# Loading x two batches at a time in a batched matmul: 32 KB per partition in one transfer, and transposes that serve both batches

## The chip, the cores and the metric

The kernel runs on one core of a Trainium2 chip. The metric is device time in microseconds (us) of one execution. The kernel before falls on two levels, 516.4 and 517.5 us, so differences under 1 us between two medians say little. The profile is one execution with the hardware profiler on; its span is 1.5 to 2 us shorter than the timed run.

Names used below: TensorE does matmuls and transposes, VectorE (DVE in the profile) and ScalarE (ACT) copy out of PSUM (the on-chip memory that TensorE writes to; the tiles of x, weights and outputs lie in another, SBUF), and GpSimd (POOL) issues most transfers. They run on sixteen DMA engines. SyncE (SP) has a second queue to the same engines. A *packet record* is one row of the trace's list of packets: start, duration, bytes written, queue. On the GpSimd queue one record is one partition's contiguous piece of a transfer.

## The reference

```python
batch, m, k, n = 32, 512, 1024, 768
x = np.random.randn(batch, m, k).astype(np.float32)
weight = np.random.randn(batch, k, n).astype(np.float32)
out = np.matmul(x, weight).astype(np.float32)
```

Per batch that is 2.10 MB of x, 3.15 MB of weight and 1.57 MB of output. Over 32 batches 218.1 MB go over HBM, the memory that holds x, weight and output.

## The kernel before

Each batch's x and weight come in one transfer each on the GpSimd queue, which casts them to bf16. TensorE transposes x in pairs of bf16 (viewed as fp32), VectorE copies the result out of PSUM, and the matmuls follow. Weights have four buffers, x has five, outputs seven. The parts that matter here, with cuts marked:

```python
w_pool = ctx.enter_context(tc.tile_pool(name="w", bufs=4))
x_pool = ctx.enter_context(tc.tile_pool(name="x", bufs=5))
...
out_pool = ctx.enter_context(tc.tile_pool(name="out", bufs=7))
tpsum = ctx.enter_context(tc.tile_pool(name="tpsum", bufs=2, space=bass.MemoryType.PSUM))
...
def load_x(b):
    xs[b] = x_pool.tile([P, MT, K], BF16, name="x_sb")
    nc.gpsimd.dma_start(out=xs[b], in_=x_view[b])
...
def transpose(b, mt):
    pt = tpsum.tile([P, JT, P], F32, name="pt")
    pairs = xs[b].bitcast(F32)
    for j in range(JT):
        nc.tensor.transpose(pt[:, j, :], pairs[:, mt, j::JT], ident)
    xT = xT_pool.tile([P, JT, P, 2], BF16, name="xT")
    nc.vector.tensor_copy(xT..., pt.bitcast(BF16)...)      # both flat: 1024 bf16
    return xT
...
# the first x, in fp32, on the SyncE queue; its last quarter in 16 pieces of 6 rows
# and one of 32
nc.sync.dma_start(x_first[:, :MT - 1], x_view[0, :, :MT - 1])
for block in range(0, 96, 24):
    for at in range(block, block + 4):
        few = slice(at, block + 24, 4)
        nc.sync.dma_start(x_first[few, MT - 1], x_view[0, few, MT - 1])
nc.sync.dma_start(x_first[96:, MT - 1], x_view[0, 96:, MT - 1])
load_w(0)
...
for b in range(1, AHEAD):          # AHEAD = 3
    load_x(b)
    load_w(b)
load_x(AHEAD)
for b in range(B):
    if b + AHEAD + 1 < B:
        load_x(b + AHEAD + 1)
    if b + AHEAD < B:
        load_w(b + AHEAD)          # from b = 1 on it waits until batch b - 1 is done
    ...                            # output of batch b - 1, on the GpSimd queue
    # transposes of tiles 0 and 1, then matmuls with those of tiles 2 and 3 between them
```

So before batch 0 is done the queue holds w0 to w3 and x1 to x5. Nothing else can be issued until the matmuls of batch 0 free the first weight buffer.

## Time and profile before

| | before |
|---|---|
| time, median | 517.36 us (516.3 to 517.5, 6 runs) |
| span of the profiled run | 515.7 us |
| HBM traffic over the span | 218.1 MB, 423 GB/s |
| TensorE busy | 417.8 us, 81% |

The list of waits of the kernel before (who waited for whom: us in total, times, longest):

```profile
POOL w_sb L62 <- PE pm L101: 66.2, 8, 35.2
...
PE pm L101 <- DMA w_sb<-in_weight_dram: 43.9, 17, 4.4
```

TensorE waits for weights.

The windows view of the kernel before, at the start and for the long middle. The columns are the window and its length, busy time (instructions) of PE, weight loads, DVE, ACT and POOL, the granted clock, the mean share of the DMA engines and GB/s. Packets of one engine overlap a little in the records, so a full engine reads 1.02.

```profile
40.00:54.00 14.00, 13.59 (x90) 9.41 (x91) 5.23 (x8) 2.34 (x4) 1.06 (x2) 1.00 1.04 219
54.00:61.00 7.00, 6.95 (x47) 4.75 (x46) 1.98 (x3) 1.28 (x3) 0.54 (x1) 1.00 1.02 214
61.00:70.00 9.00, 8.64 (x57) 5.76 (x57) 2.67 (x4) 1.65 (x3) 1.06 (x2) 1.00 1.01 249
70.00:470.00 400.00, 350.35 (x2119) 231.06 (x2157) 107.57 (x163) 62.63 (x107) 42.76 (x81) 0.95 1.02 264
```

The timeline of the kernel before (start us, duration us, what, and in brackets the idle time and what ended it): the first transposes on TensorE, and the moment at which w4 can be issued.

```profile
33.57 3.89 PE L83 MATMUL pt<-ident,x_first 128*128 128x128 f32 x16 [33.57 <-DMA x_first<-in_x_dram]
...
51.08 0.53 POOL L62 DMA_DIRECT2D w_sb<-in_weight_dram  x1 [35.18 <-PE pm L101]
```

The transfer queued last before w4 (x5) lands between 60.6 and 64.5 us, depending on the engine, so w4, issued at 51.1, comes 9 us before the first engine needs it.

### The profile page before, as it was taken

The numbers are of one execution on the slowest core, as the hardware profiler recorded it, in microseconds if no ns is written. First come the engines' busy times: TensorE is split into PE (matmuls) and PEld (weight loads), VectorE is DVE, ScalarE is ACT, GpSimd is POOL, SyncE is SP. The second block draws the span as 40 slices with busy tenths as digits, with TensorE's granted clock in tenths as the row PEclk, the third lists the DMA queues.
The fourth block names the chain that finished last, engine by engine and source line by source line (L and its number), as shares of the span: only waits on it lengthen the run. The fifth ranks groups of instructions, "written<-read, shape, count | busy, mean of one in ns | idle before, by whom it ended". The sixth has DMA issues, their size and how long they took to land.

```text
span 515.7 us, 5952 instructions
## 1 busy us (share of the span) xinstructions
PE 417.8 (81%) x2528; PEld 276.1 (54%) x2576; DVE 129.9 (25%) x196; ACT 76.2 (15%) x129; POOL 51.7 (10%) x102
## 2 busy tenths in 40 slices
PE   0039999999999988779879779887898976999990
PEld 0036666666666655446546455554564644566660
DVE  0023333333333313122223231322331322133330
ACT  0001111111111111111101111110110111111110
POOL 3000111111001010100101001100111010111000
PEclk9999999999999989899979998898997998899996
DMA  8999999999999999999999999999999999999996
GB/s 234 223 225 216 218 272 275 260 243 270 277 274 268 243 261 278 275 273 248 250 275 276 275 259 244 271 274 276 272 240 260 277 275 272 250 244 214 300 426 257
DMA packets 15097, 135.64 MB, mean 263 GB/s; under 512 B 1760, under 2 KB 1760, under 8 KB 3552
## 3 DMA queue, kind: packets, MB, share of 16 engines
q0 software_dynamic: 13824, 126.88, 96.7%
q1 hardware_dynamic: 1248, 8.39, 4.1%
q8 instruction: 20, 0.33, 0.2%
q14 instruction: 5, 0.04, 0.0%
HBM read 167.77 MB, written 50.33 MB: 423 GB/s over the span
## 4 chain that ended last, share of the span: by engine, by line
DMA 63%; PE 30%; DVE 3%; issue 1%; ACT 0%; POOLq 0%
PE pm L101 27%; DMA w_sb<-in_weight_dram 25%; DMA out_dram<-out_sb 16%; DMA x_sb<-in_x_dram 16%; DMA x_first<-in_x_dram 6%; PE pt L70 2%; DVE out_sb L113 1%; DVE xT L72 1%; PE pt L83 1%; ACT out_sb L114 0%; POOLq L144 0%; POOLq L62 0%; POOLq L56 0%
## 5 line engine op out<-in xcount | busy, mean ns | idle before, releaser
L101 PE MATMUL pm<-w_sb,xT 128*128 128x256 bf16 (+1 forms) x2000 | 363.4, 336 | 51.3 <-DMA w_sb<-in_weight_dram 43.9
L101 PEld LDWEIGHTS <-xT 128*128 128x128 bf16 x2048 | 204.5, 101 | 185.8 <-issue 52.9
L72 DVE COPY xT<-pt 128x1024 bf16<-128x1024 bf16 x124 | 82.9, 689 | 204.3 <-PE pt L70 204.3
L112 ACT COPY out_sb<-pm 128x512 f32<-128x512 f32 x64 | 37.5, 585 | 289.0 <-PE pm L101 289.0
L113 DVE COPY out_sb<-pm 128x512 f32<-128x512 f32 x64 | 44.0, 687 | 128.1 <-PE pm L101 128.1
L70 PEld LDWEIGHTS pt<-ident,x_sb 128*128 128x128 f32 x496 | 72.3, 206 | 6.0 <-issue 0.8
L70 PE MATMUL pt<-ident,x_sb 128*128 128x128 f32 x496 | 74.6, 284 | 0.0
L114 ACT COPY out_sb<-pm 128x512 f32<-128x512 f32 x64 | 37.5, 586 | 137.3 <-PE pm L101 137.2
L62 POOL DMA_DIRECT2D w_sb<-in_weight_dram x37 | 19.8, 534 | 155.7 <-PE pm L101 66.2
L56 POOL DMA_DIRECT2D x_sb<-in_x_dram x31 | 16.5, 532 | 172.9 <-DMA w_sb<-in_weight_dram 115.8
L83 PE MATMUL pt<-ident,x_first 128*128 128x128 f32 x32 | 6.0, 349 | 33.6 <-DMA x_first<-in_x_dram 33.6
L144 POOL DMA_DIRECT2D out_dram<-out_sb x28 | 15.0, 536 | 94.4 <-DMA x_sb<-in_x_dram 57.0
L83 PEld LDWEIGHTS pt<-ident,x_first 128*128 128x128 f32 x32 | 5.0, 202 | 34.2 <-issue 33.5
L84 DVE CAST xT<-pt 128x512 bf16<-128x512 f32 x8 | 5.6, 727 | 40.9 <-PE pt L83 40.7
L112 ACT ACT_TABLE_LOAD x1 | 1.3, 1283 | 0.7 <-PEq L195 0.7
masks.py:199 POOL TENSOR_SCALAR_AFFINE_SELECT ident<-ident 128x128 f32<-128x128 f32 x1 | 0.3, 287 | 0.1
masks.py:197 POOL MEMSET ident<- 128x128 f32 x1 | 0.2, 223 | 0.0
L195 POOL MEMSET const-float32-0.0<- 128x1 f32 x1 | 0.1, 98 | 0.2 <-issue 0.2
L195 POOL MEMSET const-bfloat16-1.0<- 128x1 bf16 x1 | 0.1, 101 | 0.0
L195 POOL MEMSET const-uint8-127<- 128x1 uint8 x1 | 0.1, 101 | 0.0
L195 POOL MEMSET const-float32-1.0<- 128x1 f32 x1 | 0.1, 98 | 0.0
## 6 DMA issues: line engine op xcount, KB each, us to landing
w_sb<-in_weight_dram POOLq DMA_DIRECT2D x28, 1536.0 KB, 43.2
out_dram<-out_sb POOLq DMA_DIRECT2D x28, 1536.0 KB, 41.9
x_sb<-in_x_dram POOLq DMA_DIRECT2D x31, 1024.0 KB, 39.6
w_sb<-in_weight_dram POOLq DMA_DIRECT2D x7, 768.0 KB, 31.4
out_dram<-out_sb SPq DMA_DIRECT2D x4, 768.0 KB
out_dram<-out_sb SPq DMA_DIRECT2D x2, 1536.0 KB
x_first<-in_x_dram SPq DMA_DIRECT2D x1, 1536.0 KB
w_sb<-in_weight_dram POOLq DMA_DIRECT2D x2, 384.0 KB, 28.1
```

Source lines behind the costliest of these rows:

```text
L56: nc.gpsimd.dma_start(out=xs[b], in_=x_view[b])
L62: nc.gpsimd.dma_start(out=ws[b][:, at:at + n, :], in_=w_view[b, :, at:at + n, :])
L70: nc.tensor.transpose(pt[:, j, :], pairs[:, mt, j::JT], ident)
L72: nc.vector.tensor_copy(xT.rearrange("p j m r -> p (j m r)"), pt.bitcast(BF16).rearrange("p j m -> p (j m)"))
L83: nc.tensor.transpose(pt[:, i, :], x_first[:, mt, JT * h + i::KT], ident)
L84: nc.vector.tensor_copy(xT[:, 2 * h:2 * h + 2].rearrange("p j m r -> p j r m"), pt.rearrange("p (j r) m -> p j r m", r=2),)
L101: nc.tensor.matmul(pm[bank][:, at:at + size], xT[:, ko // 2, :, ko % 2], ws[b][:, ko, off:off + size], start=(ko == 0 and not (together an ...
L112: nc.scalar.copy(o[:, 0:512], pm[0])
L113: nc.vector.tensor_copy(o[:, 512:1024], pm[1])
L114: nc.scalar.copy(o[:, 1024:N2], pm[2])
L144: nc.gpsimd.dma_start(out=out_view[at], in_=outs[at])
L195: nc = _bacc.Bacc("TRN2", target_bir_lowering=False, num_devices=1)
```

## The change

The intent: fewer and larger pieces for x. Batches 1 to 30 are loaded two at a time. Partition q then holds eight contiguous rows of one of the two batches (32 KB of fp32 in HBM), so 64 partitions belong to each batch. One transpose of a tile serves both batches, and the copy out of PSUM interleaves two tiles, so that the matmuls see the layout as before. The x pool shrinks from five single buffers to two double ones, and all transposes of a pair now stand ahead of its matmuls. The core of the diff, with cuts:

```diff
-    x_pool = ctx.enter_context(tc.tile_pool(name="x", bufs=5))
-    xT_pool = ctx.enter_context(tc.tile_pool(name="xT", bufs=8))
+    x_pool = ctx.enter_context(tc.tile_pool(name="x", bufs=2))
+    xT_pool = ctx.enter_context(tc.tile_pool(name="xT", bufs=6))
...
+    pair_view = x[1:B - 1].rearrange("(p r) (mi mo) k -> p (r mi) mo k", r=2, mo=2 * MT)
...
+    def load_pair(b):
+        xs[b] = x_pool.tile([P, 2 * MT, K], BF16, name="x_sb")
+        nc.gpsimd.dma_start(out=xs[b], in_=pair_view[b // 2])
...
+    def transpose_pair(b, mt):
+        both = xT_pool.tile([P, 2, JT, P // 2, 2, 2], BF16, name="xT")
+        for half in range(2):
+            nc.vector.tensor_copy(
+                both[:, :, :, :, half, :].rearrange("p b j i r -> p j b i r"),
+                words(b, mt + MT * half).rearrange("p j (b i r) -> p j b i r", b=2, r=2),
+            )
+        return [both[:, r].rearrange("p j i h r -> p j (i h) r") for r in range(2)]
...
-        for b in range(1, AHEAD):
-            load_x(b)
-            load_w(b)
-        load_x(AHEAD)
+        load_pair(1)
+        load_w(1)
+        load_w(2)
+        load_pair(3)
...
+            if b == 0:
+                xT = {mt: transpose_first(mt) for mt in range(MT)}
...
+                if b % 2:
+                    for mt in range(MT):
+                        ready[b, mt], ready[b + 1, mt] = transpose_pair(b, mt)
```

The load of the next pair is issued after these transposes. Before batch 0 is done the queue holds w0 to w3 and x1 to x4, one x less.

## The prediction

> **What bounds it now.** The DMA engines. The sliced page shows DMA at 9 tenths or more in all slices but the first and last, and the windows view a DMA share near 1.02 from 40 to 490 us. 218.1 MB of HBM traffic in 515.7 us is 423 GB/s; the packet records give 16384 source bytes of x every 606 ns on an engine and 24576 of weight every 907 ns: 27.2 bytes/ns and 3 to 4 ns per packet on top. Sixteen engines at that rate are 435 GB/s, the ceiling the Trainium skill states (DMA: Bandwidth & Descriptors, "Where 436 GB/s comes from"); the trace agrees. The traffic alone is then 501 us. TensorE is not the limit in the middle: the list of waits gives it 44 us of waits for weights, and the timeline repeats every 15.8 us per batch against 12.8 us of TensorE work.
>
> **What the change saves.** 8 packets less per engine and pair, 15 x 8 x 3.5 ns = 0.4 us, and 15 completions less: 1 us at most.
>
> **What it adds on VectorE and TensorE.** The copy stays 1024 bf16 elements (now 689 ns); its output comes in runs of two adjacent elements, so I expect the two-per-cycle rate to stay (VectorE: DVE Perf Modes, "Mode 2x_1P", asks for 16-bit and step 1): about 0.70 us. Eight groups of transposes now stand before the matmuls of a pair, with two PSUM buffers, so they run at the copy's pace: about 0.7 + 6 x 0.7 + 0.6 = 5.5 us per pair, against 2 x 2.4 before. With 2 x 10.4 us of matmuls TensorE needs about 26.3 us per pair; DMA needs 31.5. This hides.
>
> **What it moves: the start.** The first x comes on the SyncE queue. The packet records show each of its sixteen 6-row pieces waiting for two packets of the GpSimd queue (a piece every 2.0 us beside weights, 1.4 beside x): one packet of each queue in turn, as the skill has it (same page, "Queues, rings and completion order"). Some 32 packets pass there. Two x loads of 606 ns packets become a pair of 1209 ns packets and a weight of 907 ns: 8 x 0.60 + 8 x 0.30 = 7.2 us later. The first transpose moves from 33.6 to about 41 us. All 32 transposes of batch 0 then come first, so its last matmul ends near 58.5 instead of 50.6. Only then is weight buffer 0 free for w4. But one x transfer less is queued by then: the queue runs dry near 55 us on ten engines and 57.5 on the six that carry the small pieces. I expect idle DMA of about 3 us on those six, which set the end.
>
> **Tail.** TensorE ends some 3 us after its 503 us, under output transfers: no cost.
>
> Sum: 517.3 - 1 + 3 = 519.3 us.
>
> **Signs.** Queue packets about 11,700 instead of 13,824; first transpose at 41 us; DMA idle near 55 to 60 us; copy 0.69 to 0.75 us; steady period 31.5 us per pair; DMA full again afterwards.
>
> **What would make it wrong.** The copy losing its rate (about 1.2 us): TensorE then needs over 31.5 us per pair, some 10 to 20 us more. 32 KB pieces split in two: no start delay, about 517. A longer dry queue at the start, or a second one. The 501 us of traffic nearly exclude a 2% gain.

## More of the kernel before

The page of the kernel before: the row of tenths that the DMA engines were busy in 40 slices of the span, two queues (packets, MB, share of 16 engines' time; q0 is GpSimd's, and q8, named instruction, carries no tensor of the kernel), and one group of instructions (line, engine, operation, tiles, count | busy us, mean ns | idle time before them).

```profile
DMA  8999999999999999999999999999999999999996
...
q0 software_dynamic: 13824, 126.88, 96.7%
...
q8 instruction: 20, 0.33, 0.2%
...
L72 DVE COPY xT<-pt 128x1024 bf16<-128x1024 bf16 x124 | 82.9, 689 | 204.3 <-PE pt L70 204.3
```

The DMA engines are at nine tenths or more in all slices but the first and the last. The copy out of PSUM takes 689 ns.

The weight loads wait for TensorE mostly early on, seven of the eight times before 141 us by the timeline: the longest such wait, 35.2 us, is that of w4 for batch 0.

## The result, and the profile after

| | before | after |
|---|---|---|
| time, median | 517.36 us (6 runs) | 522.2 us (521.65 to 523.25, 6 runs) |
| ratio | | 1.0101, 95% interval 1.0087 to 1.0115 |
| span of the profiled run | 515.7 us | 520.6 us |

The page after, the lines that answer to those of before:

```profile
DMA  8999799999999999999999999999999999999996
...
q0 software_dynamic: 11664, 126.88, 95.7%
...
L84 DVE COPY xT<-pt 128x1024 bf16<-128x1024 bf16 x120 | 78.4, 688 | 35.9 <-PE pt L77 35.4
```

One slice of the DMA row fell to 7: the fifth, 52 to 65 us. There are 2160 packets fewer. The copy kept its rate, 688 ns, though it now writes runs of two elements.

The list of waits after:

```profile
POOL w_sb L69 <- PE pm L121: 183.9, 15, 53.4
...
PE pm L121 <- DMA w_sb<-in_weight_dram: 8.2, 12, 1.4
```

The wait of w4 for batch 0 grew from 35.2 to 53.4 us. TensorE's waits for weights fell, which is no gain: TensorE comes later, and its waits have partly moved to x.

The windows after:

```profile
40.00:54.00 14.00, 13.44 (x71) 9.35 (x72) 6.55 (x9) 1.17 (x2) 0.00 (x0) 1.00 1.01 216
54.00:61.00 7.00, 6.53 (x43) 4.58 (x40) 2.71 (x5) 1.17 (x2) 1.07 (x2) 1.00 0.55 92
61.00:70.00 9.00, 8.79 (x55) 6.05 (x56) 3.83 (x6) 1.17 (x2) 0.53 (x1) 1.00 0.97 205
70.00:470.00 400.00, 364.07 (x2191) 233.92 (x2189) 108.36 (x163) 64.37 (x110) 36.61 (x69) 0.97 1.02 264
```

The DMA share from 54 to 61 us is 0.55 instead of 1.02. From 61 to 70 us it is nearly full, 0.97, but moves 205 GB/s of written bytes where before moved 249 (the mix of transfers differs a little as well). From 70 us on the two kernels read the same in DMA share and GB/s.

The timeline after:

```profile
40.43 7.39 PE L103 MATMUL pt<-ident,x_first 128*128 128x128 f32 x32 [40.43 <-DMA x_first<-in_x_dram]
47.66 10.56 PE L121 MATMUL pm<-w_sb,xT 128*128 128x512 bf16 x64
...
58.52 0.53 POOL L69 DMA_DIRECT2D w_sb<-in_weight_dram  x1 [53.39 <-PE pm L121]
```

The first transpose starts 6.9 us later, all 32 transposes of batch 0 come first, and w4 is issued at 58.5 instead of 51.1 us.

By then the queue has run dry. Counted from the packet records, busy DMA engines per microsecond (up to 16.5, since records overlap):

```
from us     54    55    56    57    58    59    60    61
before    16.4  16.4  16.4  16.5  16.5  16.4  16.5  16.4
after     16.3  12.8   6.1   6.1   1.6   2.4  15.5  16.2
```

The last weight packets of ten engines end between 55.4 and 55.9 us, those of five more at about 58.1 and that of the last at 59.2, and w4's packets start at 59.8 to 60.4. So the ten are idle for about 4.2 us and the six for 1.6 on average. Averaged over all engines, and counted against sixteen busy ones, that is 3.2 us of idle time.

There is a second loss in the records. A weight packet takes 926 ns. Behind the dry stretch, w4's first packets take 1280 to 2252 ns, and its last two, at 66 to 68 us, up to 1.8 us. Adding what each GpSimd-queue packet took beyond its usual time (counting those that took over 30 ns more: the slow packets below) gives 2.0 us per engine between 50 and 70 us. Over the whole span the sum is 3.2 us, with 1.1 of it between 80 and 240 us. Before, it is 0.3 us in the whole span.

The two losses can be checked against a clock that both kernels share. When the second output has landed, both have moved the same bytes. Its sixteen engines report separately:

```
landing of the second output      first engine   mean   last engine
before, us                            87.3       88.8      91.3
after, later by                        6.3        5.2       3.1
```

The mean engine (the mean of the sixteen landing times) is 5.2 us late, and 3.2 + 2.0 is 5.2. At the 26th output (before: last engine at 492.8 us) the mean is 5.7 us late and the last engine 5.1. So the loss arose before 90 us, and it was never won back: the DMA engines stay full from there on (1.02). The step of the mean from 5.2 to 5.7 us fits the 1.1 us of slow packets after 80 us, less the half microsecond that the large packets save (see a_split1). Nothing below explains those later packets. In the repeat of this kernel (a_again) they come to 0.4 us, and the mean engine is 4.9 us late at the 26th output.

### The profile page after: what moved, and what is told of

Read it like the earlier page. It is cut to its first block, busy times and chain, and to the rows that moved or that the text cites. A ratio compares the mean times of both kernels' runs of the same rounds, so it can differ in the third digit from the quotient of the medians.

```text
span 520.6 us, 5854 instructions
## 1 busy us (share of the span) xinstructions
PE 428.8 (82%) x2576; PEld 276.4 (53%) x2576; DVE 131.1 (25%) x196; ACT 76.2 (15%) x129; POOL 43.8 (8%) x87
## 4 chain that ended last, share of the span: by engine, by line
DMA 53%; PE 37%; DVE 4%; another core or an unknown queue 2%; issue 1%; ACT 0%; POOL 0%; POOLq 0%
PE pm L121 30%; DMA w_sb<-in_weight_dram 19%; DMA x_sb<-in_x_dram 18%; DMA out_dram<-out_sb 9%; DMA x_first<-in_x_dram 8%; PE pt L77 6%; DVE xT L84 3%; PE pt L103 1%; DVE out_sb L133 1%; DVE xT L104 0%; DVE xT L92 0%; ACT out_sb L134 0%; POOL out_dram L163 0%; POOLq L163 0%
## 5 line engine op out<-in xcount | busy, mean ns | idle before, releaser
L121 PE MATMUL pm<-w_sb,xT 128*128 128x256 bf16 (+1 forms) x2048 | 338.2, 327 | 8.2 <-DMA w_sb<-in_weight_dram 8.2
L121 PEld LDWEIGHTS <-xT 128*128 128x128 bf16 x2048 | 199.5, 98 | 142.8 <-DMA w_sb<-in_weight_dram 11.4
L77 PE MATMUL pt<-ident,x_sb 128*128 128x128 f32 x496 | 86.2, 321 | 28.8 <-DMA x_sb<-in_x_dram 20.1
L84 DVE COPY xT<-pt 128x1024 bf16<-128x1024 bf16 x120 | 78.4, 688 | 35.9 <-PE pt L77 35.4
L103 PE MATMUL pt<-ident,x_first 128*128 128x128 f32 x32 | 7.3, 397 | 40.6 <-DMA x_first<-in_x_dram 40.4
L103 PEld LDWEIGHTS pt<-ident,x_first 128*128 128x128 f32 x32 | 5.5, 209 | 42.1 <-issue 40.4
L59 POOL DMA_DIRECT2D x_sb<-in_x_dram x15 | 8.0, 532 | 51.1 <-PE pt L77 26.0
L92 DVE COPY xT<-pt 128x1024 bf16<-128x1024 bf16 x4 | 2.6, 686 | 0.2 <-PE pt L77 0.2
L63 POOL DMA_DIRECT2D x_sb<-in_x_dram x1 | 0.5, 527 | 3.4 <-DMA w_sb<-in_weight_dram 3.4
```

The lines of the kernel that those rows point to most:

```text
L59: nc.gpsimd.dma_start(out=xs[b], in_=pair_view[b // 2])
L77: nc.tensor.transpose(pt[:, j, :], pairs[:, mo, j::JT], ident)
L84: nc.vector.tensor_copy(both[:, :, :, :, half, :].rearrange("p b j i r -> p j b i r"), words(b, mt + MT * half).rearrange("p j (b i r) -> ...
L92: nc.vector.tensor_copy(xT.rearrange("p j m r -> p (j m r)"), words(B - 1, mt).rearrange("p j m -> p (j m)"))
L103: nc.tensor.transpose(pt[:, i, :], x_first[:, mt, JT * h + i::KT], ident)
L121: nc.tensor.matmul(pm[bank][:, at:at + size], xT[:, ko // 2, :, ko % 2], ws[b][:, ko, off:off + size], start=(ko == 0 and not (together an ...
```

## The experiments

**Theory A:** the loss is the start alone. Large packets on the GpSimd queue hold up the small x_first pieces, the first transpose comes late, w4 comes late, the queue is empty, and the restart is slow. **Rival B:** the bunched transposes of the other pairs cost a part. **Rival C:** a late TensorE costs in itself. **Theory D**, about the slow packets: they come from engines that are in step. Eight runs were made, seven of edited kernels and one of the changed kernel again, all of them with correct results.

### First pair in two transfers (a_split1)

```diff
+        if b == 1:
+            for half in range(2):
+                rows = slice(MT * half, MT * (half + 1))
+                nc.gpsimd.dma_start(out=xs[b][:, rows], in_=pair_view[b // 2, :, rows])
+        else:
+            nc.gpsimd.dma_start(out=xs[b], in_=pair_view[b // 2])
```

> The changed kernel, but the first pair comes in two transfers of four rows, so that 606 ns packets stand again where the small x_first pieces take turns. Theory A (all of the loss is the start: late first transpose, empty queue, slow restart): first transpose back near 33.6 us, w4 issued near 51.5 us, no stretch below 14 busy DMA engines between 5 and 500 us, time 516.5 to 517.7. Rival B (the bunched transposes of the other fifteen pairs cost part of the 4.9 us): still 519 or more although the start is filled.

Measured: 516.47 us (4 runs) against 516.77 (7 runs), ratio 0.9999, interval 0.9981 to 1.0016. Its timeline:

```profile
33.40 6.97 PE L108 MATMUL pt<-ident,x_first 128*128 128x128 f32 x32 [33.40 <-DMA x_first<-in_x_dram]
...
51.08 0.53 POOL L74 DMA_DIRECT2D w_sb<-in_weight_dram  x1 [45.41 <-PE pm L126]
```

Its window, with the columns as above:

```profile
54.00:61.00 7.00, 6.81 (x45) 4.70 (x45) 2.69 (x5) 0.58 (x1) 0.53 (x1) 1.00 1.00 211
```

One transfer cut in two, out of fifteen, takes the whole loss away. All other pairs are still bunched, so rival B falls. The landings also show what the large packets save: against before, the mean engine is 0.08 us ahead at the second output and 0.59 at the 24th, which is 0.5 us for eleven pairs. (This is one trace of each. The kernel before with another start, b_noskew below, moves by 0.16 us over the same stretch with no pairs in it.)

### A fifth weight buffer (a_w5)

```diff
-    w_pool = ctx.enter_context(tc.tile_pool(name="w", bufs=4))
+    w_pool = ctx.enter_context(tc.tile_pool(name="w", bufs=5))
...
-    out_pool = ctx.enter_context(tc.tile_pool(name="out", bufs=7))
+    out_pool = ctx.enter_context(tc.tile_pool(name="out", bufs=6))
...
         load_pair(3)
+        load_w(AHEAD)
...
-            if b + AHEAD < B:
-                load_w(b + AHEAD)
+            if b + AHEAD + 1 < B:
+                load_w(b + AHEAD + 1)
```

> The changed kernel with five weight buffers (and six output buffers, to fit), so that w4 is queued from the start and need not wait for batch 0. The start stays late. Theory A: first transpose still near 40 us, no empty queue at 55 to 60 us, time 516.5 to 518. Rival C (the late start of TensorE itself costs, for instance at the tail): 520 or more. Six output buffers could cost something at the tail; the profile would show the wait.

Measured: 517.59 us (4 runs), ratio 1.0011, interval 0.9991 to 1.0031. Its first transpose in the timeline:

```profile
40.41 6.52 PE L103 MATMUL pt<-ident,x_first 128*128 128x128 f32 x28 [40.41 <-DMA x_first<-in_x_dram]
```

Its window, with the columns as above:

```profile
54.00:61.00 7.00, 6.51 (x43) 4.59 (x41) 2.74 (x5) 1.17 (x2) 1.07 (x2) 1.00 1.01 213
```

TensorE starts as late as in the changed kernel, but the queue is full and the loss is gone. Rival C falls: lateness costs nothing, emptiness does. (This run has slow packets too, 1.5 us of excess per engine, spread from 120 to 360 us. What they come from is open.)

### The kernel before with four x buffers (b_x4)

```diff
-    x_pool = ctx.enter_context(tc.tile_pool(name="x", bufs=5))
+    x_pool = ctx.enter_context(tc.tile_pool(name="x", bufs=4))
```

> The kernel before with four x buffers in place of five: x5, and behind it w4, must wait for the transposes of batch 1, so the queue runs empty at the start, without pairs, with the early first transpose and the interleaved transposes. Theory A: empty on ten engines from about 55 to 60 us, on six about 2 us, slow weight packets after it, time 520.5 to 523, as the changed kernel has. Rival B: near 517.4, since nothing of the pairs is in it.

Measured: 521.07 us (4 runs), ratio 1.0089, interval 1.0062 to 1.0115. Its window:

```profile
54.00:61.00 7.00, 7.00 (x46) 4.49 (x45) 1.98 (x3) 1.17 (x3) 1.59 (x3) 1.00 0.69 122
```

Without pairs, and with an early first transpose, one x less in the queue is enough to lose 4.3 us. By the packet records 2.1 us per engine are idle and 1.7 us are slow packets between 50 and 80 us; at the second output the mean engine is 4.0 us late. The dry stretch differs from the expected one: it ends at 58.6 to 58.8 us, so ten engines are idle for about 2.9 us, five of the six that carry the small pieces for 0.4 us and the sixth not at all. So the run lost 4.3 us although those six were hardly idle: idle time on the other ten costs.

### x_first in one piece (b_noskew and a_noskew)

```diff
-        for block in range(0, 96, 24):
-            for at in range(block, block + 4):
-                few = slice(at, block + 24, 4)
-                nc.sync.dma_start(x_first[few, MT - 1], x_view[0, few, MT - 1])
-        nc.sync.dma_start(x_first[96:, MT - 1], x_view[0, 96:, MT - 1])
+        nc.sync.dma_start(x_first[:, MT - 1], x_view[0, :, MT - 1])
```

On the kernel before:

> The kernel before with the last quarter of x_first in one transfer of 128 rows instead of seventeen small ones: no engines are held back by 2.8 us, the sixteen stay in step, and the first transpose comes near 10 us. Theory D (engines in step give slow weight packets, as after the empty queue of the changed kernel, where 8 packets took 8.9 us instead of 7.3): more slow packets than the 38 of before, time 518 to 522. Rival: the slow packets come from the restart alone; time 516.5 to 518 and few slow packets.

Measured: 516.94 us (4 runs), ratio 1.0002, interval 0.9987 to 1.0017; 57 slow packets against 38, 0.5 us of excess per engine against 0.3. There are more slow packets, as theory D expected, but they cost next to nothing and the time did not rise. Most engines (13 of 16 or more) are within about 0.6 us of each other up to 90 us, so theory D falls as stated. The run shows something else. Without the small pieces no six engines trail the rest by 2.8 us, and still the time is the same. So the trailing of these six did not set the end.

On the changed kernel:

> The changed kernel, every pair in packets of 32 KB, but the last quarter of x_first in one transfer of 128 rows, so that no chain of small pieces takes turns with the large packets. Theory A: first transpose near 10 us, w4 issued before the queue is empty, no empty stretch; the change then only saves, 0.5 us by the ledger of the run with the first pair split: 516.0 to 517.2, ratio to before 0.998 to 1.000. Rival B (pairs cost in themselves): 519 or more.

Measured: 516.07 us (6 runs) against 517.43 (11 runs), ratio 0.9988, interval 0.9974 to 1.0002. Its first transpose and w4 in the timeline:

```profile
10.33 4.57 PE L103 MATMUL pt<-ident,x_first 128*128 128x128 f32 x20 [10.33 <-DMA x_first<-in_x_dram]
...
33.83 0.53 POOL L69 DMA_DIRECT2D w_sb<-in_weight_dram  x1 [28.70 <-PE pm L121]
```

Its window, with the columns as above:

```profile
54.00:61.00 7.00, 6.91 (x44) 4.53 (x43) 1.86 (x3) 1.76 (x3) 0.53 (x1) 1.00 0.99 209
```

Here every pair is loaded as the change has it, and the loss is gone. This is the lowest median, yet its interval still holds 1.0: it is level with before, and no more.

### More small pieces (a_24)

```diff
-            for at in range(block, block + 4):
-                few = slice(at, block + 24, 4)
+            for at in range(block, block + 6):
+                few = slice(at, block + 24, 6)
```

> The changed kernel with 24 pieces of 4 rows in place of 16 of 6: sixteen more turns behind packets of the other queue, 9 of the pair (1.21 us) and 7 of weights (0.91 us), so the first transpose comes some 16 to 17 us later, near 57 us, and w4 is issued near 75 us. Theory A: the queue is empty from about 55 to 76 us on twelve engines; each further us of emptiness costs 1 us, so the time is the 522 us of the changed kernel plus about 16: 536 to 541. Rival: the wait is partly hidden, under 532.

Measured: 538.27 us (2 runs), ratio 1.0411, interval 1.0392 to 1.043. Its first transpose and w4 in the timeline:

```profile
56.93 6.51 PE L103 MATMUL pt<-ident,x_first 128*128 128x128 f32 x28 [56.93 <-DMA x_first<-in_x_dram]
...
75.01 0.53 POOL L69 DMA_DIRECT2D w_sb<-in_weight_dram  x1 [69.87 <-PE pm L121]
```

Its window, with the columns as above:

```profile
61.00:70.00 9.00, 8.79 (x52) 5.80 (x53) 4.15 (x6) 1.04 (x2) 0.00 (x0) 1.00 0.00 0
```

Eight pieces more delay the first transpose by 16.5 us and the whole kernel by 16.1 us (538.27 - 522.2). Turns behind the other queue's packets can be counted and priced: 9 x 1.21 + 7 x 0.91 is 17.3 us, a little over the 16.5 measured. Per engine 19.8 us are idle, 16.6 more than in the changed kernel, for 16.1 us of time: each idle microsecond costs about one.

### The changed kernel once more (a_again), and its first output held back (a_out2)

> The changed kernel once more, to see whether the slow packets after the empty queue come back. If they belong to the kernel: first packets of w4 at 1.4 us or more, its last two near 1.4 us on nearly all engines, about 2 us of excess per engine between 50 and 70 us. If they were chance: under 1 us of excess there. Time 521.5 to 523.5.

Measured: 521.29 us (one look, state unknown), a little under the expected range. The excess between 50 and 70 us is 1.8 us per engine, on the same packets of w4: the first (eleven of sixteen take about 1.4 us or more), and the last two. It came back, so it belongs to the kernel.

```diff
-                if b + AHEAD < B - HELD or b == B - LATE:
+                if (b + AHEAD < B - HELD and b != 1) or b == B - LATE:
```

> The changed kernel, but the first output transfer is held back by one batch, so that w4 is followed in the queue by the third pair and not by an output. The empty queue stays as it is, and so does the slow first packet. If the slow last two packets of w4 come from the output transfer behind them (theory E): they go back to 0.93 us, excess between 60 and 70 us falls from 1.2 to under 0.3 us per engine, time about 521. If they come from the restart itself: unchanged near 1.2 us, time 522. (With the pair issued at 64 us and w4 lasting to 67, the queue does not run dry again.)

Measured: 522.38 us (4 runs), ratio 1.0103, interval 1.0086 to 1.012. w4's last packets are back at 0.93 us. But w5's last two, at 84 to 86 us, directly ahead of the two outputs, are slow in their place: 0.63 us of excess from 60 to 70 us (all of it in the first packets), 1.16 us from 80 to 90. So this part of the restart's cost goes with the change from weight reads to the first output writes, and it moves with them. The time was not lower by the 1 us that theory E expected. The empty queue did not stay quite as it was either: in the profiled execution, the slowest of the four, the first transpose came at 41.3 us, w4 was issued at 59.1, and 4.0 us per engine were idle instead of 3.2. Why packets are slow at that place is not settled: engines in step are not enough (b_noskew), and in the kernel before the same place costs nothing.

## Why the prediction was right or wrong

- **The bound: right.** DMA at 1.02 from 70 to 470 us in both kernels, and each idle microsecond lengthens the run by about one (a_24). The 435 GB/s of the Trainium skill agrees as a figure only: the page counts bytes at the SBUF ports, the prediction counted bytes read, and the loads here write half as many to SBUF as they read (16 KB of 32). No run shows that the ports set this pace.
- **The saving of at most 1 us: right.** 0.5 us for eleven pairs (a_split1), though not seen in the changed kernel itself, where the later slow packets outweigh it. The per-packet cost of 3 to 4 ns behind it fits the fixed 3 cycles per packet that the Trainium skill gives (DMA: Bandwidth & Descriptors, "Why small descriptors are slow"), an estimate of 3.5 ns if they are cycles of the 850 MHz clock in its "Where 436 GB/s comes from"; the page does not say which clock it means.
- **The copy's rate: right.** 688 ns against 689.
- **The bunched transposes hide: right.** While TensorE catches up, a pair takes 26.5 us (w4 is issued at 58.5, w6 at 85.0) against 26.3 predicted, under DMA's 31.5. Cutting the first pair in two alone restores the time. Between the landings of the 2nd and the 24th output both kernels take 31.6 us per pair, with 31.5 predicted.
- **The start: right in its mechanism.** First transpose predicted at 41, measured at 40.4; end of batch 0 predicted near 58.5, measured at 58.2; dry at 55 and 57.5, measured at about 55.7 and 58.1 (one engine at 59.2).
- **The size: too small.** Predicted 519.3, measured 522.2, so +2 against +4.8 us. The step that failed is "I expect idle DMA of about 3 us on those six, which set the end". The six lost only 1.6 us of idle time, the ten lost 4.2. What counts is nearer the mean of all, 3.2 us; that this is close to the predicted 3 is luck. In b_x4 the six were idle for 0.4 us at most, and the run was still 4.3 us longer. The reason shows in the landings of the kernel before. At 70 us six engines trail by 2.7 to 3.9 us; by 408 us thirteen of sixteen are 2.5 to 5.0 us behind the first. The head start of the ten has been used up by then, so idle time on them is not free. The trace suggests what uses it up. The landings fall back in steps of about 1 us, one engine at a time, and nearly every step falls where one of the twenty 16 KB records of the queue q8 lies, each 0.88 to 0.97 us long: with the record at 424.4 us, for example, the last engine goes from 5.0 to 6.1 us behind the first. That a head start used up is the cause was read from landings; what was tested is that the six do not set the end (b_noskew, b_x4).
- **A missing term.** The restart's slow packets, 2.0 us per engine, were not in the sum. This is most of the 2.9 us that the prediction fell short. Idle 3.2 and slow packets 2.0 give the 5.2 us by which the mean engine is late at the second output. With the slow packets after 80 us (1.1) and less the saving (0.5) they give 5.8, and the mean engine is 5.7 us late at the 26th output. The time rose by only 4.8 to 4.9 us, as the last engine is 5.1 us late there.
- **The tail: right that it costs nothing.** The last copy out of PSUM starts 3.7 us later than before (506.3 against 502.7 us, with 3 predicted), under output transfers. The number is no confirmation, for the delay goes with the lost start: in a_split1, with the start filled, this copy starts at 500.4 us.

## What to carry to other kernels

Where DMA bounds a kernel from its first microsecond, ask of every change what is queued at the moment when the next issue must wait for compute, and whether it lasts until then: one transfer fewer was worth 4 us here, while a late compute engine was worth nothing. Larger packets on one queue slowed the small transfers on the other here, because the two took turns packet by packet: a small piece started every 2.6 us beside the 1.21 us packets of a pair, and every 1.4 us beside the 0.61 us packets of a single x. A saving of nanoseconds per packet is soon outweighed by one empty stretch, and a stretch that is empty on only some engines is better priced by the mean of all than by the engines that are last.

## What the Trainium skill lacked or had wrong

- DMA: Bandwidth & Descriptors, "Queues, rings and completion order": it says that an engine drains a whole packet, typically of about 9 to 17 descriptors, from one ring before it switches. Here the queues took turns after every single partition's piece (whether such a piece is one descriptor or several, the trace does not tell): a 4 KB piece and its completion each waited for one piece of the other queue, 0.61, 0.91 or 1.21 us long. With sixteen such pieces waiting, the larger pieces of the changed kernel moved the first transpose from 33.6 to 40.4 us. The page does not price this.
- The same page, "SWDGE vs HWDGE vs iDMA", gives a packet as at most 4096 bytes, preferably, and as the boundary at which an engine switches. The trace has 32 KB read and 16 KB written per partition as one record of 1227 ns, starting every 1208 ns. The small pieces beside it started every 2.59 us, so the engine did not switch inside it.
- The same page has nothing on what follows an empty queue: first packets of 1.3 to 2.3 us instead of 0.93, and the last two weight packets ahead of the first output slowed by 0.2 to 0.9 us each (together about 2.0 us per engine).
- No page puts a figure on how far engines that share a transfer evenly drift apart: from 3.9 us between the first and the last at 70 us to 6.1 us at 475 us in the kernel before, in steps of about 1 us beside the q8 records (b_noskew shows such steps too).
